# A second halved block product in Down, weight sums by DMA, another order of the products, and VectorE's order given

## The chip, the cores and the metric

The kernel runs on one core of one Trainium2 chip. The metric is the device time of one execution in microseconds (us). The core has a matrix engine (TensorE, PE in the profile; PEld is its loading of weights), VectorE (DVE), ScalarE (ACT), GpSimd (POOL) and SyncE (SP, which here only issues DMAs), an on-chip memory of 128 partitions (SBUF), accumulator banks (PSUM) that TensorE writes, and sixteen DMA engines.

## The reference

The reference is one decoder block on 1024 tokens of width 1024, in float32: a mixer (pooling and sliding-window attention, merged by gates), then a squared-ReLU MLP. The change is in the MLP's second half. What it computes:

```python
h2 = _rmsnorm(x, g_mlp_pre)
f  = jnp.square(jax.nn.relu(h2 @ w_up))      # 1024 x 4096, "Up"
ff = f @ w_down                              # 1024 x 1024, "Down"
x  = x + _rmsnorm(ff, g_mlp_post)
```

## The kernel before, in words

**Precision.** TensorE multiplies rounded float32 values here. Each operand is therefore split in two: ScalarE casts the high part (line 101), VectorE subtracts it from the value and so makes the low part (line 104). A product is three matmuls: high by high, high by low, low by high (`PASSES`).

**Down's seven products.** Down multiplies two matrices that are cut into two by two blocks: f in token halves and halves of its 4096 channels, the weights B11, B12, B21, B22 in channel halves and column halves (512 columns). Instead of eight block products it makes seven, of sums and differences of blocks. A whole product covers 512 tokens (four tiles of 128, index t), 512 columns, and 2048 channels in eight steps `s_` of 2 x 128 channels (index k2). So a step has 2 x 4 x 3 = 24 matmuls of 512 columns (`down_mm`, line 2075). The seven run in the order `PRODUCTS = (1, 5, 2, 3, 6, 7, 4)`, all eight steps of one before the next.

**Product 6 is halved.** It is made again as seven products of blocks half as large (`quarters_mm`, line 2055): 7 x 2 x 3 = 42 matmuls of 256 columns a step. It needs sums of quarter blocks of f (the e tiles, made in Up, stored to DRAM and read back), sums of quarter blocks of the weight (the T tiles, made by VectorE in `differences`), and at its end a close (`quarters_close`), in which ScalarE and VectorE join the seven results into `u4`. Three of the seven start on a PSUM bank that has been loaded with blocks of `u4`.

**Operands.** `operands(i, s_)` loads the tiles of one step and splits them; it is called two steps ahead (`AHEAD = 2`). f's blocks come from DRAM (`f_dram`), where Up has stored them along with the sums that the products need. Weights are resident (`resident`, tiles named B, 24 buffers of 4 KB a partition, pool `rp`) or streamed (`streamed`, tiles named raw, four buffers, which f, e and x1 use too). The split tiles are wh (f, six buffers) and ar (weights, six buffers). All these loads are issued on SP's queue, in the order in which the scheduler has put them.

**Weight sums before.** Product 5 uses B12 - B11 (line 1978). `differences` (lines 2005 to 2011) makes B22 - B11, B22 - B12 and the T tiles, in product 3. `last_weights` (line 2016) makes B21 less the running sum for product 4, during products 7 and 4. All are VectorE operations of 128 x 1024.

**Order.** In most of Down an automatic scheduler sets each engine's order. Given by hand are: VectorE's for what belongs to products 6, 7 and 4 (`given`), and all three engines' in the close and the last tile. Products 2 and 3 accumulate onto the banks of products 1 and 5. Up stores its results in `store` (lines 1628 to 1646), which also makes the e tiles. At Up's end its buffers give way to Down's: the memory of the pools `fp`, `gp` and others is reused for B, raw and the accumulators.

Of the kernel before, what the change touches and what calls it, by code (L numbers as in the profile page):

```python
# [14 lines left out]
P = 128  # L15
# [35 lines left out]
def block_kernel(ctx: ExitStack, tc, xt, x, consts, vecs, sinks, b_qkv, g_post, g_mlp, g_mlp_post,  # L51
# [1565 lines left out]
    def up_close0(m, f):  # L1617
# [4 lines left out]
        def store():  # L1622
# [5 lines left out]
            dve.tensor_tensor(t[:, 0, :], f[:, 512:], g[:, 512:], ALU.add)  # L1628
            dve.tensor_tensor(t[:, 1, :], t[:, 0, :], f[:, :512], ALU.subtract)
            dve.tensor_tensor(f[:, 512:], f[:, :512], f[:, 512:], ALU.subtract)  # L1630
            dve.tensor_tensor(s4, g[:, :512], t[:, 1, :], ALU.subtract)
            fd = f_dram[m // 2]
            q = nc.sync if m < NF - 2 else nc.scalar
            if m // 2 % 2 == 0:
                dve.tensor_tensor(s2[:, 256:], s2[:, :256], s2[:, 256:], ALU.subtract)
                s2_even.append(s2)
            else:
                a = s2_even.pop()
                e = g32([3, 256])
                dve.tensor_tensor(e[:, 1, :], s2[:, 256:], a[:, 256:], ALU.subtract)  # L1640
                dve.tensor_tensor(e[:, 0, :], e[:, 1, :], a[:, :256], ALU.add)
                dve.tensor_tensor(e[:, 2, :], s2[:, :256], e[:, 1, :], ALU.subtract)
                q.dma_start(e_dram(m // 4), e)
# [5 lines left out]
    stores, s2_even = [], []  # L1649

    def e_dram(s_):
        return spill[s_][:, :768].rearrange("p (a b) -> p a b", b=256)
# [284 lines left out]
    def acc4(name):  # L1937
        return [dl.tile([P, 512], F32, tag="acc", name=nm(name), bufs=12) for _ in range(4)]
# [22 lines left out]
    behind = []  # L1961

    def operands(i, s_):
# [3 lines left out]
        else:  # L1967
            ft = stage([2, 512]) if (i, s_) == (1, 3) else raw_tile()
            nc.sync.dma_start(ft, f_block(A_OF[i], s_))
            if i == 1:  # L1970
# [3 lines left out]
                wt = res["B11", s_]  # L1974
            elif i == 5:
                resident("B12", s_)
                wt = res["B11", s_]
                dve.tensor_tensor(wt, res["B12", s_], wt, ALU.subtract)
            elif i == 2:
                wt = streamed("B21", s_)  # L1980
            elif i == 3:
                resident("B22", s_)
                wt = res["B22", s_]
            elif i == 6:
                wt = res["B11", s_]
            elif i == 7:
                wt = res["B12", s_]
            else:
                wt = res["B21", s_]
        if i == 6:  # L1990
            quarters(s_, ft, wt)
            return
# [7 lines left out]
        behind[:] = [split(*wo_, wt)]  # L2000
# [12 lines left out]
    def last_weights(s_):  # L2013
        wt = res["B21", s_]
        with tc.issue_after(behind[0].ins):
            dve.tensor_tensor(wt, wt, res["B11", s_], ALU.subtract)
# [324 lines left out]
```

## Time and profile before

| | |
|---|---|
| time, median of 3 runs | 1091.01 us (1090.58 to 1097.92) |
| the profiled execution's own time | 1091.0 us |
| its span | 1089.2 us |
| mean granted TensorE clock | 0.999 |
| busy: PE, DVE, ACT, POOL | 99%, 78%, 57%, 8% |
| Down, from its first matmul to the last | 779.1 to 1081.5 us of the span |
| HBM read and written | 161.38 MB, 63.97 MB |

Times inside a profile are counted from the span's start. A row of the timeline has start, duration, engine, line, operation, the tiles written and read, their shape and a count of instructions merged in it; in square brackets stands how long the engine had been idle and what released it. A matmul's shown duration (389 ns for 512 columns) reaches past the start of the next one, so the time of a row of matmuls is read from the starts. A row of the groups has busy time and mean ns of one behind the bar, then idle time before and its releaser. SPq, ACTq and POOLq rows are DMAs issued on those engines' queues. The granted clock is given as a share of full speed.

### The profile page before, as it was taken

The numbers are of one execution on the slowest core, as the hardware profiler recorded it, in microseconds if no ns is written. First come the engines' busy times: TensorE is split into PE (matmuls) and PEld (weight loads), VectorE is DVE, ScalarE is ACT, GpSimd is POOL, SyncE is SP. The second block draws the span as 40 slices with busy tenths as digits, with TensorE's granted clock in tenths as the row PEclk, the third lists the DMA queues.
The fourth block names the chain that finished last, engine by engine and source line by source line (L and its number), as shares of the span: only waits on it lengthen the run. The fifth ranks groups of instructions, "written<-read, shape, count | busy, mean of one in ns | idle before, by whom it ended". The sixth has DMA issues, their size and how long they took to land.

```text
span 1089.2 us, 14332 instructions
## 1 busy us (share of the span) xinstructions
PE 1079.7 (99%) x5211; PEld 903.5 (83%) x5211; DVE 849.2 (78%) x1194; ACT 625.5 (57%) x1029; POOL 86.2 (8%) x142
## 2 busy tenths in 40 slices
PE   9999999999999999999999999999999999999997
PEld 8888888888888888888888888888888888898885
DVE  6688888989897887889876766665657867579996
ACT  7567886456654257567665554555446535476543
POOL 0354411100100012100000000000000000000000
PEclk9999999999999999999999999999999999999999
DMA  9666889679965776832566534445597873379622
GB/s 333 201 174 175 214 251 350 184 233 315 268 213 171 223 191 137 288 117 77 185 227 227 205 143 174 160 150 216 177 391 272 299 265 118 101 234 318 218 78 78
DMA packets 100921, 227.36 MB, mean 209 GB/s; under 512 B 10481, under 2 KB 28017, under 8 KB 100849
## 3 DMA queue, kind: packets, MB, share of 16 engines
q1 hardware_dynamic: 84416, 189.46, 50.8%
q0 software_dynamic: 10528, 16.78, 8.8%
q10 hardware_dynamic: 5904, 20.19, 4.8%
q8 instruction: 41, 0.67, 0.3%
q14 instruction: 32, 0.25, 0.1%
HBM read 161.38 MB, written 63.97 MB: 207 GB/s over the span
## 4 chain that ended last, share of the span: by engine, by line
PE 75%; DVE 4%; ACT 1%; issue 1%; DMA 1%; ACTq 0%; DVEq 0%
PE mm L583 18%; PE at L583 15%; PE at L2075 12%; PE mm L2075 11%; PE mm L1523 5%; PE mm L494 3%; PE at L2055 2%; PE at L1523 2%; PE at L1251 2%; PE mm L2055 2%; PE mm L1251 1%; PE mm L496 1%; PE at L1569 1%; DMA st<-in_w_g_dram 1%; DVE xf L2121 0%
## 5 line engine op out<-in xcount | busy, mean ns | idle before, releaser
L2075 PE MATMUL at<-ar,wh 128*128 128x512 f32 x552 | 126.0, 389 | 0.2 <-DVE ar L104 0.2
L2075 PEld LDWEIGHTS at<-ar,wh 128*128 128x128 f32 x552 | 103.4, 188 | 22.1 <-DVE ar L104 0.6
L2075 PE MATMUL mm<-ar,wh 128*128 128x512 f32 x528 | 120.5, 389 | 0.0
L2075 PEld LDWEIGHTS mm<-ar,wh 128*128 128x128 f32 x528 | 99.1, 188 | 20.5
L101 ACT CAST wh<-raw 128x1024 fp32r<-128x1024 f32 (+1 forms) x58 | 59.2, 1023 | 86.2 <-PE at L2075 37.0
L104 DVE TENSOR_TENSOR wh<-st,wh 128x512 fp32r<-128x512 f32 (+1 forms) x103 | 74.4, 733 | 38.9 <-ACT wh L101 34.3
L104 DVE TENSOR_TENSOR wh<-raw,wh 128x1024 fp32r<-128x1024 f32 (+1 forms) x58 | 68.4, 1186 | 40.8 <-ACT wh L101 40.6
L583 PE MATMUL mm<-T,wx 128*128 128x512 f32 x375 | 90.3, 389 | 0.0
L583 PEld LDWEIGHTS mm<-T,wx 128*128 128x128 f32 x375 | 70.4, 188 | 14.6
L583 PE MATMUL mm<-gr,wh 128*128 128x512 f32 x321 | 77.2, 391 | 0.0
L101 ACT CAST wh<-st 128x512 fp32r<-128x512 f32 (+2 forms) x102 | 65.8, 654 | 19.2 <-PE at L583 4.6
L583 PEld LDWEIGHTS mm<-gr,wh 128*128 128x128 f32 x321 | 59.9, 188 | 12.2
L583 PE MATMUL mm<-T,wh 128*128 128x512 f32 x267 | 66.0, 389 | 0.0
L104 DVE TENSOR_TENSOR ar<-B,ar 128x1024 fp32r<-128x1024 f32 (+2 forms) x51 | 50.9, 1011 | 14.7 <-ACT ar L101 14.4
L583 PE MATMUL at<-gr,wh 128*128 128x512 f32 x243 | 59.0, 389 | 0.0
L583 PE MATMUL mm<-x,wh 128*128 128x512 f32 x240 | 58.9, 394 | 0.0
L583 PEld LDWEIGHTS mm<-T,wh 128*128 128x128 f32 x267 | 50.1, 188 | 10.4
L101 ACT CAST ar<-B 128x1024 fp32r<-128x1024 f32 (+2 forms) x51 | 44.1, 882 | 19.3 <-PE mm L2055 6.4
L583 PEld LDWEIGHTS at<-gr,wh 128*128 128x128 f32 x243 | 45.6, 188 | 9.5
L583 PEld LDWEIGHTS mm<-x,wh 128*128 128x128 f32 x240 | 44.2, 188 | 9.6 <-ACT f L692 0.2
L583 PE MATMUL at<-T,wx 128*128 128x512 f32 x213 | 52.0, 389 | 0.0
L583 PEld LDWEIGHTS at<-T,wx 128*128 128x128 f32 x213 | 40.0, 188 | 8.3
(529 smaller groups left out, 2264.5 us busy)
## 6 DMA issues: line engine op xcount, KB each, us to landing
raw<-f_dram SPq DMA_DIRECT2D x52, 512.0 KB, 4.7
B<-in_w_dn_dram SPq DMA_DIRECT2D x32, 512.0 KB, 6.5
f_dram<-g SPq DMA_DIRECT2D x28, 512.0 KB, 2.8
st<-in_w_up_dram SPq DMA_DIRECT2D x24, 512.0 KB, 4.5
g<-spill_dram SPq DMA_DIRECT2D x17, 512.0 KB, 5.7
f_dram<-g ACTq DMA_DIRECT2D x17, 512.0 KB, 2.9
st<-in_w_g_dram SPq DMA_DIRECT2D x16, 512.0 KB, 4.7
g<-in_w_up_dram SPq DMA_DIRECT2D x15, 512.0 KB, 4.8
```

The costliest lines, as they stand in the source:

```text
L101: act.copy(hi, src)
L104: return eng.tensor_tensor(lo, src, f32(hi), ALU.subtract)
L494: pe.matmul(bs[th], whi[:, k, :], rhs(k, hl, th), start=k == 0 and hl == 0, stop=False)
L496: pe.matmul(bs[th], wlo[:, k, :], rhs(k, 0, th), start=False, stop=k == nk - 1)
L583: pe.matmul(b, w[wh][:, kt, :], x_, start=not after and kt == 0 and j == 0, stop=kt == 3 and j == 2, skip_group_check=after)
L1251: pe.matmul(b, w[wh][:, kt, :], xo[xh][:, kt, :], start=not after and kt == 0 and j == 0, stop=kt == 1 and j == 2, skip_group_check=after)
L1523: pe.matmul(bs[t], Am[a][k][ah][:, t * P:(t + 1) * P], Wm[w][k][wh], start=not after and k == 0 and j == 0, stop=k == 3 and j == 2, skip_g ...
L1569: pe.transpose(b[:, i, :], hs[4 * th + i][:, k * P:(k + 1) * P], ident)
L2055: pe.matmul(part[q][:, t, :], o[fs][fh][:, fk, t * P:(t + 1) * P], o[ws][wh][:, wk, :], start=q not in ONTO and (s_, t, j) == (0, 0, 0), s ...
L2075: pe.matmul(bs[t], fo[fh][:, k2, t * P:(t + 1) * P], wo_[wh][:, k2, :], start=not after and s2 == 0 and k2 == 0 and j == 0, stop=(s2, k2) ...
```

## The change

- Product 5 is halved as well, by the same `quarters`, `quarters_mm` and `quarters_close`, which now take the product's number. Its seven parts start on empty banks and are joined into a new tile `v4` (v's four parts).
- The order is `PRODUCTS = (1, 3, 5, 2, 6, 7, 4)`. Each whole product has its own banks (`TAGS`); products 2 and 3 no longer accumulate onto others' banks. VectorE adds product 2's bank to u, and v to c12.
- Signs of some f sums are turned (in Up's `store`, and where u, v and c12 are joined), so that the weight's running value grows by additions only: B11 + B12 (`first_sum`, VectorE), then + B22 and + B21 by accumulating DMAs on GpSimd's queue, issued behind the splits of products 5 and 6 (`quarters`); B12 + B22 by VectorE behind product 3's splits. `differences` and `last_weights` are gone. `quarter_sums` makes the T tiles, eight in product 3 for product 5 and eight in product 2 for product 6.
- B22 and B21 are streamed in products 3 and 2; neither is resident. B12's eight loads are issued in product 1, two at each of steps 1 to 4.
- Up's `store` makes e tiles for two products: one more 256-wide subtraction for each even pair and three more for each odd one, and eight more stores of 384 KB.
- VectorE's order is given by hand for the whole of Down (`down_step`); with it the squares of x1 move from product 5 to product 7, c11's gain and square from product 2's end to product 6, the roots of the first four tiles to product 7's step 5, and their output to the last two steps of product 7 and the first two of product 4.

```diff
@@ store (Up) @@
-            dve.tensor_tensor(t[:, 0, :], f[:, 512:], g[:, 512:], ALU.add)
+            dve.tensor_tensor(t[:, 0, :], f[:, 512:], g[:, 512:], ALU.subtract)
...
-            dve.tensor_tensor(s4, g[:, :512], t[:, 1, :], ALU.subtract)
+            dve.tensor_tensor(s4, g[:, :512], t[:, 1, :], ALU.add)
...
-                dve.tensor_tensor(s2[:, 256:], s2[:, :256], s2[:, 256:], ALU.subtract)
-                s2_even.append(s2)
+                for s in (t[:, 0, :], s2):
+                    dve.tensor_tensor(s[:, 256:], s[:, :256], s[:, 256:], ALU.subtract)
+                s_even.append(t)
...
+                t0 = s_even.pop()
+                for k, s in enumerate((t[:, 0, :], s2)):
+                    a, e = t0[:, k, :], g32([3, 256])
+                    dve.tensor_tensor(e[:, 1, :], s[:, 256:], a[:, 256:], ALU.subtract)
+                    dve.tensor_tensor(e[:, 0, :], e[:, 1, :], a[:, :256], ALU.add)
+                    dve.tensor_tensor(e[:, 2, :], s[:, :256], e[:, 1, :], ALU.subtract)
+                    q.dma_start(e_dram(5 + k, m // 4), e)
@@ operands @@
+            wt = (streamed("B21", s_) if i == 2 else streamed("B22", s_) if i == 3 else
+                  res["B12" if i == 7 else "B11", s_])
+        if i in HALVED:
+            quarters(i, s_, ft, wt)
+            nc.gpsimd.dma_start(wt, w_block("B22" if i == 5 else "B21", s_), accum_op=ALU.add)
             return
...
+        if i == 3:
+            w12 = res["B12", s_]
+            dve.tensor_tensor(w12, w12, wt, ALU.add)
...
-    def differences(s_):
-        b11, b12, b22 = (res[n, s_] for n in ("B11", "B12", "B22"))
-        dve.tensor_tensor(b11, b22, b11, ALU.subtract)
-        w = halved(b11)
-        dve.tensor_tensor(b12, b22, b12, ALU.subtract)
+    def first_sum(s_):
+        w11 = res["B11", s_]
+        dve.tensor_tensor(w11, w11, res["B12", s_], ALU.add)
+
+    def quarter_sums(s_):
+        w = halved(res["B11", s_])
         tt = res["T", s_] = rp.tile([P, 4, 256], F32, tag="w", name=nm("T"))
...
-    def last_weights(s_):
-        wt = res["B21", s_]
-        with tc.issue_after(behind[0].ins):
-            dve.tensor_tensor(wt, wt, res["B11", s_], ALU.subtract)
@@ the products' loop @@
-    PRODUCTS = (1, 5, 2, 3, 6, 7, 4)
+    PRODUCTS = (1, 3, 5, 2, 6, 7, 4)
+    HALVED = (5, 6)
...
+    def down_step(j, i, s_):
+        last = s_ == NS - 1
+        if i in HALVED and last:
+            with tc.manual_schedule(engines=CORE):
+                quarters_mm(i, s_)
+                quarters_close(i)
+        if i == 2 and last:
+            down_mm(i, s_, banks[i], False, [(s_, k2, t) for k2 in range(2) for t in range(4)])
+            for t in range(4):
+                dve.tensor_tensor(c11[t], u[t], banks[i][t], ALU.add)
+        if j + AHEAD < len(steps):
+            operands(*steps[j + AHEAD])
+        if i in HALVED:
+            if not last:
+                quarters_mm(i, s_)
+            if i == 6 and 1 <= s_ < 5:
+                fin_half(s_ - 1, 0, c11[s_ - 1])
+            return
...
+        if i == 1 and 1 <= s_ < 5:
+            for s2 in (2 * s_ - 2, 2 * s_ - 1):
+                resident("B12", s2)
+        if 4 <= j < 4 + NS:
+            first_sum(j - 4)
+        if i == 3:
+            quarter_sums(s_)
+        if i == 2:
+            quarter_sums(s_)
+            if 1 <= s_ < 5:
+                dve.tensor_tensor(c12[s_ - 1], c12[s_ - 1], v[s_ - 1], ALU.add)
         if i == 7:
+            if s_ < 4:
+                after_sixth(s_)
+                square_x1(2 * s_)
+                square_x1(2 * s_ + 1)
+            elif s_ == 5:
+                first_roots()
+        if NS * 5 + 6 <= j < NS * 5 + 10:
+            fin_out(j - NS * 5 - 6, (c11, c12))
...
+    with tc.manual_schedule(engines={mybir.EngineType.DVE}):
+        for j in range(1, AHEAD):
+            operands(*steps[j])
+        for j, step in enumerate(steps):
+            down_step(j, *step)
```

More of the change, by code (lines that the diff above doesn't have):

```diff
@@ L1937, in acc4 @@
     def acc4(name):
-        return [dl.tile([P, 512], F32, tag="acc", name=nm(name), bufs=12) for _ in range(4)]
+        return [dl.tile([P, 512], F32, tag="acc", name=nm(name), bufs=8) for _ in range(4)]
     def raw_tile_of(shape):
@@ L1959, in streamed @@
         return t
-    behind = []
     def operands(i, s_):
@@ L2256, in block_kernel @@
                     down_mm(i, s_, bs, False, late[:-2], late[-3])
-                    with tc.manual_schedule(engines={mybir.EngineType.PE, mybir.EngineType.DVE,
-                                                     mybir.EngineType.Activation}):
+                    with tc.manual_schedule(engines=CORE):
                         last_tile(i, n, bs[t], late[-2:])
```

163 lines of the change are left out of this document (53 added, 110 removed).

## The prediction, made before the changed kernel ran

> **What bounds the kernel now.** I read the page first: its busy line, the chain that ended last, the costliest groups.
>
> ```profile
> PE 1079.7 (99%) x5211; PEld 903.5 (83%) x5211; DVE 849.2 (78%) x1194; ACT 625.5 (57%) x1029; POOL 86.2 (8%) x142
> PE 75%; DVE 4%; ACT 1%; issue 1%; DMA 1%; ACTq 0%; DVEq 0%
> ```
>
> TensorE is busy 99% of the span and the chain runs mostly over its matmuls. So only two things count: how much matmul time the change takes away, and whether it makes TensorE wait. For the first I read TensorE's timeline through Down.
>
> ```profile
> 784.58 38.24 PE L2075 MATMUL at<-ar,wh 128*128 128x512 f32 x168
> ...
> 909.70 43.68 PE L2075 MATMUL mm<-ar,wh 128*128 128x512 f32 x192
> 953.22 3.04 PE L2055 MATMUL at<-ar,wh 128*128 128x256 f32 x24
> ...
> 988.65 1.60 PE L2055 MATMUL at<-ar,wh 128*128 128x256 f32 x12
> 990.09 0.88 PE L2055 MATMUL mm<-ar,wh 128*128 128x256 f32 x6
> ...
> 993.69 6.58 PE L2075 MATMUL at<-ar,wh 128*128 128x512 f32 x28
> 1000.47 37.47 PE L2075 MATMUL at<-ar,wh 128*128 128x512 f32 x164 [0.21 <-DVE ar L104]
> 1037.78 28.72 PE L2075 MATMUL mm<-ar,wh 128*128 128x512 f32 x126
> ```
>
> The starts matter. A whole product (here the fourth, product 3) takes 953.22 - 909.70 = 43.52 us: 192 matmuls, 226.7 ns each, 5.44 us a step of 24. The halved product 6 takes 993.69 - 953.22 = 40.47: twelve matmuls of 256 columns take 990.09 - 988.65 = 1.44, so 120 ns each, and 42 a step 5.04, eight steps 40.32. So it lost 0.15 to waits. The product behind it takes 1037.78 - 993.69 = 44.09, 0.57 over 43.52: the price of closing the halved product.
>
> The windows give the other engines' room, by product.
>
> ```profile
> 700.26:738.34 38.08, 38.08 (x169) 31.54 (x168) 23.75 (x38) 20.12 (x32) 0.00 (x0) 1.00 0.45 163
> ...
> 866.20:909.70 43.50, 43.50 (x193) 36.03 (x192) 32.30 (x33) 18.44 (x23) 0.00 (x0) 1.00 0.72 237
> 909.70:953.20 43.50, 43.50 (x193) 36.05 (x192) 29.62 (x39) 20.20 (x29) 0.00 (x0) 1.00 0.33 100
> 953.20:993.70 40.50, 40.50 (x338) 40.37 (x337) 32.36 (x38) 31.64 (x44) 0.00 (x0) 1.00 0.78 255
> 993.70:1037.80 44.10, 43.89 (x195) 35.91 (x194) 42.79 (x57) 23.30 (x31) 0.00 (x0) 1.00 0.73 253
> ```
>
> The columns are length, PE, PEld, DVE, ACT, POOL, granted clock, DMA share, GB/s. The clock is full throughout. VectorE has room in Up (23.75 of 38.08) and in product 6 (32.36 of 40.50), little in product 7 (42.79 of 44.10).
>
> **The change part by part.**
>
> *Product 5 halved.* Eight steps fall from 5.44 to 5.04: -3.20. I add the 0.15 that product 6 lost, and a close of its own.
>
> The Trainium skill, "TensorE: Matmul & The Clock Gate", section "Wait — 56ns, not 53.3ns?", gives a warm matmul N / 2.4 GHz plus about 2.5 ns, as an estimate 109.2 ns for 256 columns and 215.8 for 512. By that the eight steps would save 4.7 us instead of 3.2. The trace has 120 and 226.7, and decides.
>
> *The close.* It holds up the operands of the next product's second step, which VectorE's order puts behind it:
>
> ```profile
> 993.15 0.68 DVE L2062 TENSOR_TENSOR st<-st,at 128x512 f32<-128x512 f32 x1
> ...
> 997.46 0.68 DVE L2069 TENSOR_TENSOR u<-u,st 128x512 f32<-128x512 f32 x1
> 998.06 1.22 DVE L104 TENSOR_TENSOR wh<-raw,wh 128x1024 fp32r<-128x1024 f32 x1
> ...
> 999.20 1.22 DVE L104 TENSOR_TENSOR ar<-B,ar 128x1024 fp32r<-128x1024 f32 x1
> ```
>
> Eight additions, then the two splits, done at 1000.42; that is the wait of 0.57. The new close has seven additions, 0.6 less; (2,1) is queued behind it. Bounds 0 and 0.57; I take the row's 0.57.
>
> *VectorE's additions.* The groups from Up's end on (the fourth those of product 6 alone), and the DMA issue of x1:
>
> ```profile
> L1978 DVE TENSOR_TENSOR B<-B,B 128x1024 f32<-128x1024 f32 x8 | 9.8, 1220 | 0.9 <-DMA B<-in_w_dn_dram 0.9
> ...
> L2009 DVE TENSOR_TENSOR T<-B 128x512 f32<-128x512 f32 x8 | 5.5, 690 | 0.2
> ...
> L2010 DVE TENSOR_TENSOR T<-B,T 128x256 f32<-128x256 f32 x8 | 3.4, 422 | 0.2
> ...
> L104 DVE TENSOR_TENSOR wh<-raw,wh 128x768 fp32r<-128x768 f32 x7 | 6.7, 956 | 4.9 <-ACT wh L101 4.9
> ...
> L2104 ACT ACTIVATE raw<-raw 128x1024 f32<-128x1024 f32 x8 | 8.5, 1060 | 4.8 <-DMA raw<-x_dram 4.8
> ...
> raw<-x_dram SPq DMA_DIRECT2D x8, 512.0 KB, 5.1
> ```
>
> A whole weight sum is 1.22, a set of quarter sums 0.69 + 2 x 0.42 = 1.53. Four whole sums a step index go (L1978, L2005, L2007, L2016: 39), two come (`first_sum`, the one behind product 3's split: 20), the quarter sums double (+12), and sixteen sums go to DMAs. The halved product's splits take 0.96 + 1.22 + 0.69 + 0.42 + 1.22 = 4.5 a step against 2 x 1.22: 2.1 more, 17. In Up each two pairs get four more 256-wide operations, 4 x 0.42 = 1.7 in 38.08, where VectorE is idle for 14.3: nothing, hidden by the matmuls; without that cover it would be at most 8 x 1.7 = 13. The extra e tile (8 stores, 384 KB) goes on SP before t and f; nobody reads it until product 5.
>
> *Where VectorE's given order is densest.* In the first half of product 3 a step asks for three whole operations (two splits, one sum), a `first_sum` and the quarter sums: 3 x 1.22 + 1.22 + 1.53 = 6.4 against 5.44; over four steps 3.9 late. Operands are made two steps ahead (10.9), so 3.9 is covered unless VectorE comes in late; then the splits of (3,5) and on stand behind sums, and TensorE waits for them. Bounds 0 and 3.9; I take 0, as product 7 ran at 42.79 of 44.10 with no wait but the close's. Product 6 gets four gain multiplications (0.69 each) and four squares, into 8 us of idle VectorE: nothing. Product 7 loses `last_weights` and gets eight x1 squares on ScalarE, which has 20.8 idle there; their loads share the four raw slots with f: three loads a step, 5.1 to land and 1.06 to square, 6.2 each, are 19 us of slot against 4 x 5.44 = 22, just enough.
>
> *The sums by DMA.* Sixteen accumulates of 512 KB on GpSimd's queue, idle in Down. The nearest row is that of the eight accumulating loads at L1430 (least, median, most):
>
> ```profile
> DMA to landing us min/median/max: 5.9/6.8/8.3
> ```
>
> 6.8 us to land. Product 5's are read a product later, product 6's two later: over 30 us of cover. Nothing; without cover each would be 6.8.
>
> *B12's loads move into product 1.* All eight are now issued at its steps 1 to 4. Here I read SP's queue, its waits, ScalarE's waits for data and the window of those steps.
>
> ```profile
> SPq L1953 <- PE at L2075: 9.5, 1, 9.5
> ...
> 784.77 0.93 SPq L1953 DMA_DIRECT2D B<-in_w_dn_dram  x2
> ...
> 795.91 1.05 ACT L101 CAST wh<-raw 128x1024 fp32r<-128x1024 f32 x1 [4.38 <-DMA raw<-f_dram]
> 797.59 1.05 ACT L101 CAST ar<-B 128x1024 fp32r<-128x1024 f32 x1 [0.63 <-DMA B<-in_w_dn_dram]
> ...
> 804.43 1.05 ACT L101 CAST wh<-raw 128x1024 fp32r<-128x1024 f32 x1 [1.73 <-DMA raw<-f_dram]
> 805.82 1.05 ACT L101 CAST ar<-B 128x1024 fp32r<-128x1024 f32 x1 [0.34 <-DMA B<-in_w_dn_dram]
> ...
> 798.67 1.23 DVE L104 TENSOR_TENSOR ar<-B,ar 128x1024 fp32r<-128x1024 f32 x1 [0.46 <-ACT ar L101]
> ...
> 802.73 1.23 DVE L104 TENSOR_TENSOR ar<-B,ar 128x1024 fp32r<-128x1024 f32 x1
> ...
> 809.57 1.23 DVE L104 TENSOR_TENSOR ar<-B,ar 128x1024 fp32r<-128x1024 f32 x1
> ...
> 795.50:801.00 5.50, 5.50 (x26) 4.57 (x25) 2.45 (x2) 2.76 (x3) 0.00 (x0) 1.00 1.05 394
> ```
>
> The DMA engines are full (share 1.05) and hand over a 512 KB load each 805.82 - 804.43 = 1.39 us. Operands of (1,4) are split at 799.9; that step starts at 784.58 + 3 x 5.44 = 800.9: 1.0 us to spare. Those of (1,5) are split at 804.0 for 806.3 (2.3 to spare), of (1,7) at 810.8 for 817.2 (6.4). Two B12 loads ahead of f(4) and B11(4) put them 2.8 later: TensorE waits 1.8. With all eight in the written order, two ahead of each of steps 4 to 7, eight loads put (1,7) back by 11.1, so TensorE loses 11.1 - 6.4 = 4.7 in all. On the other side, SP's queue stood 9.5 us at the first B load, behind product 1's first step, until 784.77; a few loads issued into that hole would cost nothing. Ends 0 and 4.7. I take 1.8: the first pair stands in the way, and the later steps have 2.3 to 6.4 to spare for the rest.
>
> **The sum**, against the profiled execution's 1091.0 (span 1089.2 and 1.8 around it; the median is 1091.01): -3.20 + 0.15 + 0.57 + 1.8 = -0.7, so 1090.3.
>
> **The rivals.**
>
> 1. *The loads are free.* If B12 goes into the hole ahead of 784.77, or behind product 1's own loads, only -2.5 is left: 1088.5. For it: SP idle 9.5 us; against: what held it was a buffer still in use by (1,0).
> 2. *Slower: the whole backlog.* SP keeps the written order and TensorE waits at (1,4) to (1,7): -2.5 + 4.7, 1093.2; it decides the sign from 2.5 us of waiting on. For it: the share of 1.05 and two loads with each step; against: SP's hole.
> 3. *VectorE's given order binds.* Its lateness of 3.9 in product 3 meets late loads and passes the cover: 1090.3 + 3.9 = 1094.2. For it: 6.4 against 5.44; against: two steps of lead.
> 4. *The accumulates cost the engines double.* Product 6's share of 0.78 plus 8 x 1.39 / 40.5 = 0.27 would be 1.05, and f and e would come late: 2 us, 1092.3. For it: nothing measured here, the landing of 6.8 is that of a plain load in a busy stretch; against: B21's loads leave that window. The Trainium skill, "DMA: Bandwidth & Descriptors", section "Issuing engines are not separate DMA queues", says that all queues share the same 16 engines, so by it GpSimd's queue is no way round.
>
> **How the numbers follow.** Chances: forecast 0.35, rival 1 0.3, rival 2 0.2, rival 3 0.1, rival 4 0.05. The range reaches from below rival 1 (a close at nothing) to past rival 3: 1087.6 to 1095. A change under 1% (10.9 us) can't be told from none; every case lies within it, so same has 0.96, slower 0.03 (rivals 2 and 3 together and worse), faster 0.01.
>
> **What would show it.** TensorE's timeline: L2055 twice, 40.3 to 40.5 each. Right on the loads: ScalarE's casts in product 1 waiting for B and raw, TensorE waiting before (1,4), one to two us. Rival 1: no wait ahead of product 3; rival 2: waits at each of four steps; rival 3: TensorE waiting for VectorE's splits in products 3 and 5; rival 4: ScalarE waiting for raw in product 6. The prediction is wrong if a buffer's release in the crowd at Up's end holds SP for longer than now, which would add to product 1, or if Up gets waits.

## The result, and the profile after

The changed kernel takes 1102.42 us (median of 7 runs, 1100.91 to 1105.25) where the kernel before takes 1091.01 (7 runs, 1090.58 to 1097.92): a ratio of 1.0099, 95% interval 1.0076 to 1.0123. I forecast 1090.3 and a range up to 1095. The profiled execution took 1102.42 with a span of 1100.6, 11.4 more than before's 1089.2. From the page, the busy line and the chain that ended last:

```profile
PE 1082.3 (98%) x5355; PEld 907.5 (82%) x5355; DVE 875.1 (80%) x1273; ACT 634.6 (58%) x1046; POOL 105.0 (10%) x158
...
PE 80%; DMA 8%; DVE 7%; ACT 3%; issue 2%; SPq 0%; DVEq 0%; ACTq 0%
```

The chain now runs through DMAs for 8% (1% before) and VectorE for 7% (4% before). The windows show where, by product in the new order 1, 3, 5, 2, 6, 7 (length, PE, PEld, DVE, ACT, POOL, clock, DMA share, GB/s):

```profile
778.53:825.54 47.01, 45.35 (x194) 35.57 (x193) 25.54 (x29) 18.39 (x20) 0.00 (x0) 1.00 0.92 331
825.54:869.05 43.51, 43.51 (x193) 36.04 (x192) 43.10 (x50) 19.31 (x23) 0.24 (x1) 1.00 0.65 193
869.05:911.04 41.99, 41.35 (x338) 40.51 (x336) 32.24 (x43) 28.25 (x40) 7.02 (x6) 1.00 0.88 225
911.04:957.44 46.40, 44.34 (x194) 36.00 (x193) 40.49 (x55) 19.33 (x22) 3.61 (x3) 1.00 0.79 231
957.44:999.74 42.30, 41.20 (x337) 40.59 (x336) 36.99 (x47) 31.86 (x49) 6.04 (x5) 1.00 0.96 274
999.74:1049.10 49.36, 45.15 (x194) 35.67 (x193) 36.32 (x52) 31.50 (x46) 2.41 (x2) 1.00 0.85 258
```

The clock is full, so every lengthening is waiting. Against before: product 1 +3.49 (43.52), 5 -1.53 (43.52), 2 +2.88 (43.52), 6 +1.83 (40.47), 7 +5.27 (44.09), 3 unchanged; with Down starting 0.61 earlier, product 4 0.55 longer and the end 0.47 shorter, this makes the 11.4. What releases TensorE stands in brackets in its timeline:

```profile
807.32 6.09 PE L2070 MATMUL at<-ar,wh 128*128 128x512 f32 x24 [0.64 <-ACT ar L101]
814.14 11.55 PE L2070 MATMUL at<-ar,wh 128*128 128x512 f32 x48 [0.74 <-ACT ar L101]
...
913.43 0.74 PE L2070 MATMUL mm<-ar,wh 128*128 128x512 f32 x2 [1.90 <-DVE ar L104]
...
984.64 1.58 PE L2044 MATMUL mm<-ar,wh 128*128 128x256 f32 x11 [0.92 <-DVE ar L104]
...
1019.21 0.73 PE L2070 MATMUL at<-ar,wh 128*128 128x512 f32 x2 [1.15 <-DVE ar L104]
...
1026.03 0.74 PE L2070 MATMUL at<-ar,wh 128*128 128x512 f32 x2 [1.08 <-DVE ar L104]
...
1032.84 0.74 PE L2070 MATMUL at<-ar,wh 128*128 128x512 f32 x2 [1.03 <-DVE ar L104]
```

In these rows it is late operands each time; a bank shows in one short wait only (0.29 us at product 7's start, for the close's addition at L2056). Three places, so three questions: product 1; products 5, 2 and 6 together; product 7.

### The profile page after: what moved, and what is told of

Its sections match the earlier page's. It is cut to its first block, busy times and chain, and to the rows that moved or that the text cites. A ratio compares the mean times of both kernels' runs of the same rounds, so it can differ in the third digit from the quotient of the medians.

```text
span 1100.6 us, 14826 instructions
## 1 busy us (share of the span) xinstructions
PE 1082.3 (98%) x5355; PEld 907.5 (82%) x5355; DVE 875.1 (80%) x1273; ACT 634.6 (58%) x1046; POOL 105.0 (10%) x158
## 4 chain that ended last, share of the span: by engine, by line
PE 80%; DMA 8%; DVE 7%; ACT 3%; issue 2%; SPq 0%; DVEq 0%; ACTq 0%
PE mm L583 26%; PE at L583 18%; PE mm L2070 6%; PE mm L1523 5%; PE at L2070 4%; PE mm L494 3%; PE mm L191 2%; PE mm L182 2%; PE sc L182 2%; PE at L1523 2%; PE at L1251 2%; DMA raw<-spill_dram 2%; DVE wh L104 2%; DVE ar L104 2%; DMA B<-in_w_dn_dram 2%
## 5 line engine op out<-in xcount | busy, mean ns | idle before, releaser
L2070 PE MATMUL at<-ar,wh 128*128 128x512 f32 x468 | 116.9, 393 | 5.6 <-DVE ar L104 3.9
L2070 PEld LDWEIGHTS at<-ar,wh 128*128 128x128 f32 x468 | 87.0, 188 | 27.7 <-DVE ar L104 7.1
L2070 PE MATMUL mm<-ar,wh 128*128 128x512 f32 x420 | 103.5, 391 | 2.4 <-DVE ar L104 2.1
L101 ACT CAST wh<-raw 128x1024 fp32r<-128x1024 f32 (+1 forms) x66 | 64.8, 995 | 69.0 <-DMA raw<-f_dram 41.9
L104 DVE TENSOR_TENSOR wh<-raw,wh 128x1024 fp32r<-128x1024 f32 (+1 forms) x66 | 76.2, 1156 | 30.3 <-ACT wh L101 30.1
L2070 PEld LDWEIGHTS mm<-ar,wh 128*128 128x128 f32 x420 | 78.6, 188 | 19.9 <-DVE ar L104 2.8
L1978 POOL DMA_DIRECT2D B<-in_w_dn_dram x16 | 19.3, 1208 | 515.3 <-PE mm L2070 385.3
L2044 PE MATMUL mm<-ar,wh 128*128 128x256 f32 x336 | 47.0, 284 | 1.1 <-DVE ar L104 1.1
L104 DVE TENSOR_TENSOR ar<-B,ar 128x1024 fp32r<-128x1024 f32 (+2 forms) x51 | 39.6, 803 | 10.6 <-ACT ar L101 10.2
```

What stands on the lines that cost most here:

```text
L101: act.copy(hi, src)
L104: return eng.tensor_tensor(lo, src, f32(hi), ALU.subtract)
L1978: nc.gpsimd.dma_start(wt, w_block("B22" if i == 5 else "B21", s_), accum_op=ALU.add)
L2044: pe.matmul(part[q][:, t, :], o[fs][fh][:, fk, t * P:(t + 1) * P], o[ws][wh][:, wk, :], start=q not in onto and (s_, t, j) == (0, 0, 0), s ...
L2070: pe.matmul(bs[t], fo[fh][:, k2, t * P:(t + 1) * P], wo_[wh][:, k2, :], start=not after and s2 == 0 and k2 == 0 and j == 0, stop=(s2, k2) ...
```

## The experiments

All start from the changed kernel. A single run scatters by more than a microsecond (the changed kernel's own seven span 4.3), so I read single runs by the starts of the products in TensorE's timeline, which show to 0.1 us where the time went. A product's length is from its first matmul's start to that of the next product.

Two cautions go with that. A product that waits scatters from run to run: product 1 took 45.74 to 47.19 in the changed kernel and the five runs whose edits come behind it. So a difference of a microsecond in a waiting product of a single run shows nothing by itself. And in six single runs the granted clock fell in one product: to 0.96 in product 2 (gain later, no x1), to 0.96 or 0.97 in product 7 (plain loads, five buffers, T sums later), to 0.91 in product 5 (automatic order). With five buffers it was 0.55 for the 3.8 us behind a wait of 2.69, and nine matmuls took 3.75 us there instead of 2.04; in each of the first five runs such a stretch adds 1.5 to 1.7 us to the product. The clock of the changed kernel, of the kernel before and of the last version was full in each product.

| run | time | 1 | 3 | 5 | 2 | 6 | 7 |
|---|---|---|---|---|---|---|---|
| before | 1091.0 | 43.52 | 43.52 | 43.52 | 43.52 | 40.47 | 44.09 |
| changed | 1102.4 | 47.01 | 43.51 | 41.99 | 46.40 | 42.30 | 49.36 |
| B12 late | 1101.1 | 43.52 | 44.49 | 41.71 | 45.65 | 42.49 | 50.59 |
| gain later | 1101.4 | 47.19 | 43.51 | 41.56 | 47.22 | 42.59 | 45.64 |
| no x1 | 1098.6 | 45.74 | 43.52 | 42.39 | 47.42 | 42.43 | 45.05 |
| no accumulates | 1094.6 | 47.14 | 43.52 | 40.63 | 44.27 | 40.70 | 45.30 |
| plain loads instead | 1100.9 | 45.96 | 43.52 | 42.92 | 45.73 | 42.47 | 48.04 |
| five raw buffers | 1100.0 | 46.24 | 43.52 | 40.64 | 44.20 | 40.71 | 51.82 |
| product 5 whole | 1100.4 | 46.04 | 43.52 | 43.52 | 43.52 | 42.51 | 48.79 |
| automatic order | 1107.3 | 54.07 | 43.53 | 54.14 | 43.69 | 40.42 | 44.87 |
| three together | 1094.7 | 43.52 | 44.46 | 40.62 | 43.60 | 40.68 | 48.91 |
| x1 in 3 and 2 | 1091.0 | 43.52 | 44.49 | 40.63 | 43.95 | 41.91 | 44.10 |
| x1 in 2 | 1094.2 | 43.95 | 44.72 | 40.63 | 46.50 | 42.03 | 44.09 |
| T sums later | 1100.3 | 43.52 | 43.77 | 43.65 | 45.39 | 42.53 | 48.86 |
| the same, with x1 | 1092.9 | 43.52 | 43.77 | 42.80 | 45.27 | 40.69 | 44.10 |
| the same, x1 in 3 | 1090.9 | 43.52 | 43.76 | 42.80 | 44.12 | 40.70 | 44.14 |
| x1 in 3, T sums as changed | 1090.3 | 43.52 | 44.48 | 41.66 | 43.63 | 40.69 | 44.10 |
| first sums earlier | 1093.9 | 43.52 | 46.01 | 41.96 | 45.24 | 40.68 | 44.13 |
| copies behind | 1088.6 | 43.52 | 43.52 | 40.56 | 43.60 | 40.67 | 44.07 |
| the same, last x1 in 2 | 1088.9 | 43.52 | 43.52 | 40.63 | 43.97 | 40.70 | 44.10 |

Times of the changed kernel, of the kernel before, of "the same, with x1" and of the last four are medians of 7 to 11 runs, the others single runs; before, beside the single runs, took 1090.4 to 1090.7.

### Product 1: B12's loads

In the changed kernel, SP's queue and ScalarE's timeline in product 1 show the theory:

```profile
775.97 14.34 SPq L1955 DMA_DIRECT2D B<-in_w_dn_dram  x4
791.19 0.37 SPq L1969 DMA_DIRECT2D raw<-f_dram  x1
792.34 3.52 SPq L1955 DMA_DIRECT2D B<-in_w_dn_dram  x4
```

```profile
798.15 1.05 ACT L101 CAST wh<-raw 128x1024 fp32r<-128x1024 f32 x1 [8.32 <-DMA raw<-f_dram]
...
804.91 1.05 ACT L101 CAST wh<-raw 128x1024 fp32r<-128x1024 f32 x1 [4.42 <-DMA raw<-f_dram]
...
811.71 1.05 ACT L101 CAST wh<-raw 128x1024 fp32r<-128x1024 f32 x1 [4.45 <-DMA raw<-f_dram]
```

Between one load of f and the next stand weight loads, and f comes in every 6.8 us, where TensorE needs it every 5.44. The edit gives B12 to the steps after these:

```diff
-        if i == 1 and 1 <= s_ < 5:
-            for s2 in (2 * s_ - 2, 2 * s_ - 1):
+        if i == 1 and 4 <= s_ < 8:
+            for s2 in (2 * s_ - 8, 2 * s_ - 7):
```

> The changed kernel with B12's eight loads issued at steps 4 to 7 of product 1 instead of 1 to 4. Theory A (these loads stand ahead of product 1's own operands in a queue whose engines are full): product 1 falls from 47.0 us to 43.5 to 44.5 and the time by 2.5 to 3.5, to some 1099. Rival A2 (the wait only moves: the sums that need B12 come late, VectorE enters product 3 late, and products 3 to 6 pay): product 1 falls, the products behind it grow by as much, the time stays at 1102.

Measured: 1101.13. Its windows of products 1 and 3:

```profile
779.25:822.77 43.52, 43.52 (x193) 36.04 (x192) 23.40 (x27) 16.39 (x18) 0.00 (x0) 1.00 0.97 358
822.77:867.26 44.49, 44.16 (x193) 35.81 (x192) 44.08 (x51) 20.35 (x25) 0.00 (x0) 1.00 0.58 180
```

Product 1 is back at 43.52, with the same loads and a fuller DMA (0.97 against 0.92): it was the order in the queue. But the time fell by 1.3 only. Product 3 now loses 0.97, with VectorE busy for 44.08 of 44.49, and product 7 takes 1.2 more, which is within its scatter. I read the first as VectorE's density (my third rival) with the lead gone that product 1's wait had given it; that was half of it, as the last experiments show.

### Product 7: two engines in fixed order

The changed kernel's timelines of ScalarE and of VectorE (two fences) at the first of product 7's waits:

```profile
1011.27 1.06 ACT L2099 ACTIVATE raw<-raw 128x1024 f32<-128x1024 f32 x1 [3.86 <-DMA raw<-x_dram]
...
1014.39 1.06 ACT L2099 ACTIVATE raw<-raw 128x1024 f32<-128x1024 f32 x1
...
1015.45 0.62 ACT L2076 ACTIVATE junk<-c 128x512 f32<-128x512 f32 x1
```

```profile
1010.28 0.69 DVE L2168 TENSOR_TENSOR v<-v,u 128x512 f32<-128x512 f32 x1
1016.19 0.69 DVE L2079 TENSOR_TENSOR c<-c,bc 128x512 f32<-128x512 f32 x1 [5.22 <-ACT junk L2076]
1016.80 1.22 DVE L104 TENSOR_TENSOR wh<-raw,wh 128x1024 fp32r<-128x1024 f32 x1
1017.93 1.22 DVE L104 TENSOR_TENSOR ar<-B,ar 128x1024 fp32r<-128x1024 f32 x1
```

ScalarE's squares of x1 (L2099) wait for their load, and the square of c12 (L2076), whose input was there, stands behind two of them. VectorE's next operation in the given order is the gain (L2079), which overwrites c12 after that square. It idles for 5.22 us, the two splits behind it come late, and TensorE starts at 1019.21 as the second one ends. The waits of product 7 in the changed kernel, then in the one before:

```profile
DVE c L2079 <- ACT junk L2076: 10.8, 4, 5.2
...
ACT raw L2099 <- DMA raw<-x_dram: 6.2, 4, 3.9
```

```profile
DVE c L2084 <- ACT junk L2081: 0.3, 1, 0.3
```

First edit: VectorE's gain comes two steps later.

```diff
@@ after_sixth @@
-        fin_half(t, 1, c12[t])
+        fin_sq(t, 1, c12[t])
@@ product 7 @@
+            if 2 <= s_ < 6:
+                fin_gain(1, c12[s_ - 2], c12[s_ - 2])
```

> The changed kernel with one thing moved: the gain multiplication of each c12 tile in product 7 is placed two steps later in VectorE's order than its square on ScalarE. Theory B (in product 7 VectorE, in its given order, stands behind a square that ScalarE does only after x1 squares, which wait for their loads; the splits behind it come late): product 7 falls from 49.4 us to 44 to 46, the time by 3 to 5, to some 1098. Rival B2 (x1's loads themselves hold up f's, by buffers or by the DMA engines): product 7 stays at 48 to 49.4 and the time within 1 us.

Second edit: the squares of x1 and their loads are left out.

```diff
-                square_x1(2 * s_)
-                square_x1(2 * s_ + 1)
```

> The changed kernel without x1's eight loads and squares in product 7 (left out: the sums of squares of x1 are set to one). Theory B (ScalarE, waiting in its queue at an x1 square for its load, keeps back the close's copy and the c12 squares, and VectorE's given order stands behind them): product 7 falls from 49.4 us to 44 to 45, the time by 4 to 5. Rival (product 7 waits for its own f loads, for buffers or DMA engines filled by others): product 7 stays above 47.

Measured: product 7 falls to 45.64 with the gain later (1101.35) and to 45.05 without x1 (1098.64). Without x1, VectorE's wait for the square is nearly gone; from its waits in product 7:

```profile
DVE c L2079 <- ACT junk L2076: 1.3, 4, 0.5
```

Taking away either link takes away most of the loss: the late load ahead of the square on one engine, or the fixed place of the gain on the other. A third run below takes it away too, so the two are not the whole of it. With the gain later the time fell by 1.1 only, though product 7 fell by 3.7: products 2, 6 and 4 took 0.8, 0.3 and 1.2 more. Product 2's share goes with its clock of 0.96 (nine matmuls took 3.26 us there, 2.13 in the changed kernel, behind waits of 1.79 and 1.90); why the other two grew is not shown.

### Products 5, 2 and 6: the accumulates

Without the sixteen accumulates:

```diff
-            nc.gpsimd.dma_start(wt, w_block("B22" if i == 5 else "B21", s_), accum_op=ALU.add)
```

> The changed kernel without the sixteen accumulating DMAs (left out: B22 and B21 are not added to the running weight sum, so products 6 and 4 use other weights). Theory C2 (these 8 MB fill the DMA engines in products 5 and 6, and e and f come late): products 5, 2 and 6 fall from 130.7 us to 126 or less. Theory C (four raw buffers, released late by VectorE): they stay within 1 us of 130.7. The time falls by 4 or stays.

Measured: 1094.62. Products 5, 2 and 6 take 125.6 together, against 130.7 with the accumulates, and product 1 keeps its 47.14. The DMA issues in product 5, in the changed kernel and without accumulates (size, median us to landing):

```profile
q0 software_dynamic: 1428, 2.76, 40.9%
...
raw<-f_dram SPq DMA_DIRECT2D x7, 512.0 KB, 5.7
B<-in_w_dn_dram POOLq DMA_DIRECT2D x6, 512.0 KB, 7.8
raw<-spill_dram SPq DMA_DIRECT2D x6, 384.0 KB, 5.1
```

```profile
raw<-f_dram SPq DMA_DIRECT2D x8, 512.0 KB, 4.3
raw<-spill_dram SPq DMA_DIRECT2D x6, 384.0 KB, 3.0
```

Product 7 falls to 45.30, although x1's squares and the gain stand where they stood. VectorE still waits 6.9 us for the square of c12 (10.8 with the accumulates), but x1's loads land sooner; in product 7 of the changed kernel and of this run:

```profile
raw<-x_dram SPq DMA_DIRECT2D x6, 512.0 KB, 6.2
```

```profile
raw<-x_dram SPq DMA_DIRECT2D x6, 512.0 KB, 4.7
```

The changed kernel issues two of the accumulates as late as product 7. So they are a third link of its loss; how much is theirs alone no run separates.

Back in product 5, beside accumulates a load of e needs 5.1 us instead of 3.0, one of f 5.7 instead of 4.3. Is it that an accumulate occupies the DMA engines for longer than its bytes? Then plain loads of the same blocks into the same buffers would cost less.

```diff
-            nc.gpsimd.dma_start(wt, w_block("B22" if i == 5 else "B21", s_), accum_op=ALU.add)
+            nc.gpsimd.dma_start(wt, w_block("B22" if i == 5 else "B21", s_))
```

> The changed kernel with the sixteen accumulating DMAs turned into plain loads of the same 512 KB to the same place, on the same queue (left out: the addition, so later weights differ). Theory: an accumulate holds the DMA engines longer than its bytes (product 5's share is 0.88 of 42.0 us with six of them and 0.55 of 40.6 without, some 2.4 us each, where a plain load takes 1.4): product 5's share falls to 0.75 or so, and products 5, 2 and 6 from 130.7 us to 127 to 128. Rival: it is the bytes: the share stays at 0.85 or more and the three products at 130 or more.

Measured: 1100.93, and 131.1 for the three products. Its window of product 5 and its issues there:

```profile
868.64:911.56 42.92, 41.46 (x338) 40.62 (x336) 32.90 (x43) 28.78 (x40) 5.43 (x8) 1.00 0.75 251
```

```profile
q0 software_dynamic: 1071, 3.93, 30.4%
...
B<-in_w_dn_dram POOLq DMA_DIRECT2D x8, 512.0 KB, 5.4
...
raw<-spill_dram SPq DMA_DIRECT2D x6, 384.0 KB, 5.4
```

The engines are less full (0.75 against 0.88), and nothing is gained. An accumulate does hold them nearly twice as long for its bytes (in 42 us 40.9% for 2.76 MB against 30.4% for 3.93 MB), but that isn't the cost. (The rows say how: 1428 packets against 1071, 0.19 us of an engine's time for each in both runs, but 1.9 KB in one of an accumulate and 3.7 KB in a plain one.) What stays the same is that e takes 5 us to land beside another 512 KB. A load can be issued when one of the four raw buffers is free, and that sets how early. So, a fifth:

```diff
-        return dl.tile([P] + shape, F32, tag="raw", name=nm("raw"), bufs=4)
+        return dl.tile([P] + shape, F32, tag="raw", name=nm("raw"), bufs=5)
```

> The changed kernel with five raw buffers instead of four. Theory C (with four buffers a load can be issued only when VectorE, late in its given order, has released the buffer of two steps ago, so lateness is handed on through the loads): products 5, 2 and 6 together fall from 130.7 us (42.0, 46.4, 42.3) to 125 to 127, and the time by 3 to 6. Rival C2 (the DMA engines are too full in these products, by the accumulating DMAs): the three products stay within 1 us of 130.7.

Measured: 1099.95. With the accumulates in place, products 5, 2 and 6 take 125.6 (40.64, 44.20 and 40.71), as without them. A window of product 5:

```profile
869.30:909.90 40.60, 40.60 (x337) 40.38 (x336) 34.49 (x44) 29.51 (x42) 7.03 (x6) 1.00 0.91 240
```

The share is 0.91 and TensorE shows no idle time: the fullness costs nothing once loads go out early enough. Half of the 5 us came back at once in product 7 (51.82), where the queue of x1 now holds up the close's copy (L2052) and the clock fell behind that wait, as said above; TensorE's timeline of this run:

```profile
998.38 3.91 PE L2070 MATMUL mm<-ar,wh 128*128 128x512 f32 x9 [2.69 <-ACT st L2052]
```

To see what halving product 5 is worth in the changed kernel, I made it whole again. It then reads f in the form stored for the halved product, with differences of quarters in it.

```diff
-    HALVED = (5, 6)
+    HALVED = (6,)
```

> The changed kernel with product 5 made whole again (24 matmuls of 512 columns a step, no close, no e loads, no quarter sums for it), all else as changed. If halving product 5 brings its 3.2 us and the losses come from the rest of the rearrangement, the time rises by 1.5 to 3 to some 1105. If halving brings its losses with it (its close, its loads and sums make products 5, 2 and 3 wait): product 5 takes 43.5, product 2 falls from 46.4 to 43.5 to 44.5, and the time falls by 1 to 2 to some 1101.

Measured: 1100.39. Product 5 takes 43.52, and product 2, behind it, falls from 46.40 to 43.52: in the changed kernel the halving, with its loads of e and its T sums, gains 1.5 in product 5 and loses 2.9 in product 2. The accumulates run in product 5 here as well, and the packets of their queue hold the DMA engines for 51.6% of the product, yet TensorE doesn't wait: the accumulates cost where the halved product's loads of e come beside them.

### The given order itself

```diff
-    with tc.manual_schedule(engines={mybir.EngineType.DVE}):
+    with nullcontext():
```

> The changed kernel with VectorE's order left to the scheduler in all of Down (the close and the last tile keep theirs). If the given order is what makes lateness (it puts sums ahead of splits that are due), products 3, 5, 2 and 6 lose their waits and the time falls by 4 to 7. If the order matters little beside buffers and loads, the time stays within 2; it can rise, since the scheduler's own estimates decide.

Measured: 1107.33. Product 5 takes 54.14, with a clock of 0.91. (Product 1's 54.07 counts from one matmul that the scheduler put ahead of Up's last ones; from its second, at 779.79, it is 48.13.) The automatic order is worse by 4.9, so the hand-given order as a whole isn't the fault. But products 2, 6 and 7 take 43.69, 40.42 and 44.87 under it, near the kernel before, and in product 7 VectorE waits 0.9 us for the square instead of 10.8, with x1's squares still there: the given order is a part of the loss in product 7, and the automatic one has its own in product 5.

### All together, and what is left

B12 late, the gain later and five buffers:

> Three edits together: B12's loads at steps 4 to 7, the gain two steps behind its square, five raw buffers. If the losses add up as the single runs say (product 1 3.5, products 5, 2 and 6 5.2, product 7 3.7 of which the close's late copy may give back 2 to 3): span 1088 to 1091, time 1090 to 1093, level with before. If they stand in for one another, the time stays above 1096.

Measured: 1094.71. Products 1, 5, 2 and 6 are mended, product 3 keeps 44.46 and product 7 48.91, where TensorE again waits for the close's copy (2.17 us). So the gain's place doesn't mend product 7 once there are five buffers, and x1 must leave it. With B12 late, five buffers and the gain where it was, its squares at every second step of products 3 and 2 (and then, with B12 one step earlier, all in product 2):

```diff
+        if i in (3, 2) and s_ % 2 == 0:
+            square_x1(s_ // 2 + (4 if i == 2 else 0))
```

> The changed kernel with B12's loads at steps 4 to 7, five raw buffers, and x1's loads and squares moved from product 7 to the even steps of products 3 and 2. If product 7's waits are those of ScalarE behind x1's loads: product 7 near 45 us, the other products as in the run of three edits (43.5, 44.5, 40.6, 43.6, 40.7), time 1090 to 1091, level with before. If x1 does the same harm wherever it stands: products 3 and 2 grow by 2 each and the time stays at 1093 or more.

> The same with x1 at every step of product 2 alone, and B12's loads at steps 3 to 6 of product 1. Product 3, which lost 0.9 with the loads at steps 4 to 7, should be back at 43.5 to 44 and product 1 at 43.5; product 2, with three loads a step through five buffers beside the last accumulates, at 43.6 to 45. Time 1089.5 to 1092; by the rival 1093 or more.

Measured: 1091.03 and 1094.19. In both, product 7 takes 44.1 as before the change. All of x1 in product 2 costs 2.5 there (46.50 against 43.95), and with either product 6 takes 41.91 or 42.03 instead of 40.68. With B12 one step earlier product 3 didn't come back as forecast (44.72), and product 1 took 43.95.

What is left is product 3's loss. If it is VectorE's density there, the T sums for product 5 should leave it: they come four steps later, with B12 late,

```diff
+        if NS + 4 <= j < 2 * NS + 4:
+            quarter_sums(j - NS - 4)
...
-        if i == 3:
-            quarter_sums(s_)
```

> The changed kernel with B12's loads at steps 4 to 7 of product 1, as once before, and product 5's quarter sums made four steps later in VectorE's order (second half of product 3 and first half of product 5). Theory D (with product 1 no longer waiting, VectorE's dense order in product 3's first half, 6.4 us of work a step of 5.44, makes TensorE wait there): product 3 falls from 44.5 us to 43.5 to 43.7. Rival D2 (product 3 waits for its streamed loads): it stays at 44.3 or more.

and the same with five buffers and x1 in products 3 and 2 (then at every step of 3):

> Four edits: B12's loads at steps 4 to 7, five raw buffers, x1 at the even steps of product 3 and the first four of product 2, the quarter sums four steps later. If every loss named so far is gone, the products take 43.5, 43.5, 40.7, 43.6, 40.7, 44.1 and 42.6: 2.1 us less than before's seven (300.8), so 1088.5 to 1089.5, a ratio of 0.998 to 0.999. If halving product 5 brings waits of its own that none of these edits touches, 1090.5 or more.

> The same four edits with x1 at all eight steps of product 3. Product 2 and product 6's start are then free of x1: 43.6 and 40.7; product 3 has three loads a step through five buffers: 43.5 if the buffers do, 44.5 or more if not. Time 1088.5 to 1090.5.

Measured: 1100.28, 1092.9 (10 runs, 1090.77 to 1094.69; ratio 1.002, interval 1.001 to 1.0029) and 1090.85. Product 3 falls to 43.77, but product 5, where half of the T sums went, takes 42.80 instead of 40.63: moved, not gained, and the second of these runs missed its forecast of 1088.5 to 1089.5. With the T sums left in product 3, and B12 late, five buffers and x1 at every step of product 3:

> Three edits: B12's loads at steps 4 to 7, five raw buffers, x1 at every step of product 3; the quarter sums where the change has them. The quarter sums then cost product 3 about 1 us (44.5) instead of product 5 2.2: products 43.5, 44.5, 40.6, 43.6 to 44.1, 40.7, 44.1, 42.6, 1.5 less than before's sum of 300.8: 1088.8 to 1090, ratio 0.998 to 0.9995. If product 3 pays for x1 as well (45.5 or more): 1090.5 to 1091.5, no difference.

Measured: 1090.27 (10 runs, 1089.23 to 1091.66; before beside it 1090.77), a ratio of 0.9997, interval 0.9987 to 1.0006: no difference from before, and just above its forecast. Next, the same with `first_sum` two at a time, to take VectorE's work out of product 3:

```diff
-        if 4 <= j < 4 + NS:
-            first_sum(j - 4)
+        if 5 <= j < 9:
+            first_sum(2 * j - 10)
+            first_sum(2 * j - 9)
```

> The same, with the first sums (B11 + B12) two at a time at steps 5 to 8 of the whole order, so that VectorE does them in product 1, where it idles, and not in product 3's first half. If VectorE's dense order is all that product 3 pays for: product 3 at 43.5 to 43.7, 1087.8 to 1089. If VectorE then stands at these sums waiting for B12's loads, with splits behind them: products 1 or 3 lose 1 to 3 us, 1090 or more.

Measured: 1093.86 (7 runs; ratio 1.0027, interval 1.0016 to 1.0038), worse, with 46.01 in product 3. This miss showed the cause. VectorE's timeline in this run, the splits of the streamed weight in product 3's first steps:

```profile
822.37 1.23 DVE L104 TENSOR_TENSOR ar<-raw,ar 128x1024 fp32r<-128x1024 f32 x1 [5.73 <-ACT ar L101]
...
828.05 1.22 DVE L104 TENSOR_TENSOR ar<-raw,ar 128x1024 fp32r<-128x1024 f32 x1
```

It stands still for 5.73 us before product 3, and in its order no `first_sum` may pass; then a step asks it for 828.05 - 822.37 = 5.68 us against 5.44. The run without this edit (x1 in 3, T sums as changed) has the same hold, and ScalarE's timeline there says why:

```profile
814.02 1.06 ACT L101 CAST wh<-raw 128x1024 fp32r<-128x1024 f32 x1 [3.03 <-DMA raw<-f_dram]
820.57 0.59 ACT L2241 COPY u<-at 128x512 f32<-128x512 f32 x1 [5.49 <-PE at L2070]
821.05 1.05 ACT L101 CAST ar<-raw 128x1024 fp32r<-128x1024 f32 x1
```

The copy of product 1's first bank into `u`, which must wait until that bank is complete, stands ahead of the cast of product 3's first weight. ScalarE's order is the automatic one; in the changed kernel the copies came behind the first three of these casts (at 823.70, the casts at 819.84 to 822.52). The run with B12 late alone has the hold too: its first copy starts at 820.93 after 5.40 us of waiting, with the cast behind it. So the copies are put behind the casts of product 3's first two steps:

```diff
@@ split @@
-            act.copy(hi, src)
+            casts.append(act.copy(hi, src))
@@ product 1's end @@
-                act.copy(u[t], bs[t])
+                with tc.issue_after(casts[-1].ins):
+                    act.copy(u[t], bs[t])
```

> The best version so far, with ScalarE's four copies of product 1's results (its banks into u) put behind the casts of product 3's first two steps; before, the first copy stood ahead of three of these casts, waited 5.5 us for the end of product 1, and VectorE waited 5.8 us behind it. If product 3's loss of 0.97 comes from that hold (VectorE enters product 3 with no lead), product 3 takes 43.5 to 43.7 instead of 44.48, product 5, which VectorE then enters earlier, up to 0.5 less than its 41.66, and the time is 1088.8 to 1089.6. If VectorE's density alone makes it, product 3 stays at 44.4 and the time at 1090.3.

and, beside it, the last square of x1 moved out of the border between products 3 and 5:

> The kernel of the run beside it (copies behind), with the last square of x1 moved from product 3's last step, where it stands ahead of casts of product 5, to product 2's step 4. If that square makes product 5's loss of 1.06, product 5 takes 40.6 to 41.0 and the time falls by 0.5 to 1 below that of the run beside it; if it is VectorE's lateness out of product 3, product 5 stays as in that run, and the time is the same within 0.3.

Measured: 1088.62 (11 runs, 1088.01 to 1089.33; before beside it 1090.89), ratio 0.9979, interval 0.997 to 0.9988, and 1088.93 (11 runs; 0.998, 0.9971 to 0.9989). The windows of the first, products 3, 5 and 2:

```profile
822.91:866.43 43.52, 43.52 (x193) 36.04 (x192) 41.61 (x49) 27.25 (x38) 0.57 (x1) 1.00 0.86 288
866.43:906.99 40.56, 40.56 (x337) 40.41 (x336) 34.68 (x44) 31.60 (x44) 6.68 (x6) 1.00 0.95 249
906.99:950.59 43.60, 43.60 (x195) 35.98 (x193) 37.88 (x53) 17.40 (x20) 3.61 (x3) 1.00 0.82 243
```

Both losses are gone, product 3's 0.96 and product 5's 1.10, with T sums and x1 where they were. VectorE starts to split that first weight 5.55 us ahead of product 3 instead of 0.3; from VectorE's timeline of the first (line 104 is 106 here):

```profile
817.36 1.22 DVE L106 TENSOR_TENSOR ar<-raw,ar 128x1024 fp32r<-128x1024 f32 x1
```

The density needs a lead, and has it. The last square of x1 plays no part: product 5 doesn't gain (40.63), product 2 loses 0.37. The version with the copies behind the casts, 1088.62, beats both kernels, the one before by 0.2%.

## Why the prediction was wrong

**Right: the matmul work.** Where neither loads nor VectorE are late, product 5 takes 40.56 to 40.64, 2.9 less than before; I had -3.20 + 0.15 = -3.05. Against the 0.57 for the close, product 2 loses 0.68 with five buffers alone, 0.75 without accumulates and 0.08 in the last version. Up costs nothing that shows: Down starts 0.61 earlier here, and between 778.5 and 779.9 over the runs with the given order, 779.14 before.

**Mis-sized: B12's loads.** I took 1.8; they cost 3.49 in the profiled execution (2.2 to 3.7 over the runs that leave them there). My argument was that only the first pair stands in the way. The traces show the mechanism of rival 2, a wait at step after step, at three quarters of its 4.7. The step that failed is the choice by spare time per operand: with f coming in every 6.8 us against 5.44, each step eats the spare time of the next.

**Failed: the sums by DMA at nothing.** I asked when the sums are needed (30 us later) and not whom their transfers delay. They cost 5.1 us over products 5, 2 and 6 and had a part in product 7's loss. That is the place of rival 4, at a chance of 0.05 and a price of 2, but not its mechanism: plain loads of the same bytes cost the same, and a fifth buffer removes it with the accumulates in place. The term is a load's landing, 3.0 to 5.1 us, against the lead that four buffers allow, and it needs the halved product's own loads beside it: with product 5 whole the accumulates cost nothing there. By the Trainium skill, "DMA: Bandwidth & Descriptors", section "Issuing engines are not separate DMA queues", GpSimd's queue is no way round; the trace agrees, since loads of e on SP's queue took 5.1 us beside accumulates on GpSimd's and 5.4 beside plain loads there.

**Failed: x1's squares in product 7 at nothing.** Product 7 holds the largest term, 5.27. It isn't the squares' alone: it falls to 45.05 without them, but also to 45.64 with the gain later and to 45.30 without accumulates. I compared slots (19 us of 22) and ScalarE's idle time (20.8), and both say it fits. The slots were short by the landing: with x1 landing in 6.2 us instead of 5.1, three loads come to 3 x (6.2 + 1.06) = 21.8 of 22. And what decided was the order: I did not ask what is queued behind a waiting square on ScalarE, and who waits for that on VectorE. The Trainium skill, "TensorE: Matmul & The Clock Gate", section "Architectural detail: the array is 16× 32×32, not 1× 128×128", calls ScalarE's and VectorE's queues strictly first in, first out. The trace agrees: c12's square started at 1015.45, behind two squares of x1, though VectorE had gone on from c12 to its next subtraction, L2168, at 1010.28.

**Half right: VectorE's density in product 3.** I took 0 for two steps of lead, "unless VectorE comes in late". The changed kernel shows 0 (43.51). With B12 late VectorE does come in late, behind ScalarE's copy, and it costs 0.97, inside my bounds of 0 and 3.9; with the copies behind the casts it is 0 again. The clause was right; I had not looked for what could make it late.

**What the sum would have been.** With the four repairs the span is 1086.7, 2.5 less than before: -2.96 in product 5, +0.20 in product 6, +0.08 in product 2, +0.25 in Down's start. The halving is worth what its matmuls say. That the time, 1088.62, meets rival 1's 1088.5 is in part luck: its condition was another (B12's loads in SP's hole), and 0.49 less for the close makes up for product 6 and Down's start. The changed kernel lies 13.9 us above this version, all of it waits, of which I had priced 1.8. Against the forecast's -0.7 it lies 12.1 off, and the three steps above make this up: 1.7 too little for B12's loads, 5.1 in products 5, 2 and 6, 5.3 in product 7.

## What to carry to other kernels

A transfer or an operation that is needed late is not free for that: ask which load it stands beside or ahead of, and how many buffers that load has in hand. Where engines run in fixed orders, idle time on one is no measure of room; follow what is queued behind each instruction that may wait, and who waits for that. A wait that is taken away can uncover the next one of the same kind, so look at every product's start after each repair before calling the rest a lack of throughput.

## What the runs showed of the hardware

An accumulating DMA into SBUF held the DMA engines for 40.9% of 42 us for 2.76 MB, plain loads for 30.4% for 3.93 MB: 1.9 times as long for a byte, at 0.19 us a packet in both, with 1.9 KB in an accumulate's packet and 3.7 KB in a plain one. It took 7.8 us to land against 5.4, and 5.8 where product 5 was whole and no loads of e ran beside it. The landing of a 384 KB load went from 3.0 to 5.1 or 5.4 us beside 512 KB transfers on another queue, alike at a DMA share of 0.88 and of 0.75.

The granted clock fell to 0.55 for 3.8 us behind a wait of TensorE of 2.69 us, and nine matmuls of 512 columns took 3.75 us instead of 2.04. Waits of 1.79 to 2.60 us in four more runs were followed by such a stretch; waits of 1.90 (changed kernel) and 2.60 us (B12 late) were not. What decides between the two is not shown.
